# Spreading the middle stage of long convolutions through an attention, with loads a task ahead and stores a task late

## The chip, the cores and the metric

The kernel runs on one core of a Trainium2 chip. The core has a matrix engine (TensorE, PE in the profile; its weight loads are shown as PEld), a vector engine (VectorE, DVE), a scalar engine (ScalarE, ACT), a general engine (GpSimd, POOL) and SyncE (SP), which here only issues DMA transfers. Each engine works through its own queue in order, and semaphores let one wait for another. Products accumulate in PSUM banks of 128 × 512 numbers of 32 bits, working tiles lie in SBUF, everything else in the chip's DRAM. The metric is the device time of one execution, in microseconds; less is better.

## The reference

One encoder layer on 2048 rows of 1024 numbers. The input is projected; a part of the columns goes to an attention of 8 heads, another to a "Hyena" group, which passes a sequence twice through a long two-sided filter and a gate. Both results are normalised, put side by side and projected again; routed experts follow.

```python
def attend(blk):
    qn, qr = blk
    s = jnp.einsum('bqhd,bkhd->bhqk', qn, k_nope) + jnp.einsum('bqhr,bkr->bhqk', qr, k_rope)
    p = jax.nn.softmax(s.astype(jnp.float32) * scale, axis=-1).astype(v.dtype)
    return jnp.einsum('bhqk,bkhd->bqhd', p, v)
...
for o in range(HYENA_ORDER):
    zf = z.astype(jnp.float32)
    y = jnp.fft.irfft(jnp.fft.rfft(zf, n=2 * S, axis=1) * filt_f[:, o], n=2 * S, axis=1)[:, :S]
    z = (parts[o + 1].astype(jnp.float32) * (y + zf * hyena_bias[o])).astype(hy_raw.dtype)
```

The change touches only how these two are laid side by side. What is computed stays the same.

## The kernel before, in words

**The attention** (`attention`) goes through 32 blocks: 8 heads, each in 4 quarters of 512 queries. A block (a round, below) is 16 steps, one for each 128 keys. A step makes the scores (three products, `s`), two exponentials on ScalarE (`eh`, and the full value over `s`), the remainder `el` on VectorE, a sum over steps on GpSimd (`acc`), and two products with the values (`o`, `l`) for the step two before. In between stands work for the next block: one or two `max_step`, each a product `x` and a maximum on VectorE (`mx`), 16 in a block; at step 14 `max_row`, which reduces these maxima to one number for a query (`nm`), copies it to column 96 of `mz`, transposes `mz` with four products and has ScalarE put the row into the next block's queries; and at step 9 `query`, the queries of the block after the next. `free_sums` and `close_block` end the block before at steps 1 and 3. The next block's scores need the row that `max_row` makes.

**The convolutions** (`hyena`, one generator) run beside it: at each step of the attention it gets 0.7 of a turn (`drive`), and one PSUM bank, `h`. Each of the two orders `o` has four kinds of tasks, over two halves `i` of the channels: `spectrum` (the filter's spectrum, `F_dr`), `fwd1` (first products of the transform, into `Ad`), a middle stage (`first_half`: products with `zm`, the multiplication with the spectrum on VectorE (`pr`) and GpSimd (`zs`, `y`); `second_half`: products with `ivm`, into `Bd`), and `inv` (last products and the gate `tb`, into `Z1` or `HY`). The order is plain: all of `spectrum`, all of `fwd1`, the whole middle stage of both halves, all of `inv`, and the same for the second order. Each task issues its loads where it starts and its store where it ends, on SyncE's queue.

**What sets the order on an engine.** The code is written in the order of these turns, and a scheduler places the instructions of each engine from it, with the buffers and banks as limits. So instructions written apart can stand side by side in the end. Tiles named `ta`, `tb`, `tc` are the convolutions' three kinds of buffers (3, 2 and 2 of each).

Of the kernel before, what the change touches and what calls it, by code (L numbers as in the profile page):

```python
# [11 lines left out]
F32 = mybir.dt.float32  # L12
# [36 lines left out]
def hybrid_layer(ctx, tc, I, out):  # L49
# [581 lines left out]
    def hyena(hp, hw, bk):  # L631
# [7 lines left out]

        def fwd1(o, i, q4):  # L640
# [3 lines left out]
            zt = hw.tile([128, 4, HC], F32, name="tb")  # L644
            SY.dma_start(zt, ZS[o][:, q4 * 4:q4 * 4 + 4, hc])
            for q2 in range(2):
                ev = hw.tile([128, 2, 2, HC], F32, name="tc")
                for qq in range(2):
                    ql = q2 * 2 + qq
                    p = bk("h")  # L650
                    for mt in range(2):
                        T.matmul(p[:, mt * HC:(mt + 1) * HC], w1c[:, ql, mt * 128:mt * 128 + 128], zt[:, ql, :],
                                 start=True, stop=True)
                    A.activation(ev[:, :, qq, :], p.rearrange("p (m c) -> p m c", m=2), AF.Copy)
                    if qq == 0:
                        yield
                for mt in range(2):
                    q0 = q4 * 4 + q2 * 2
                    SY.dma_start(Ad[2 * o + i][mt * 128:mt * 128 + 128, q0:q0 + 2, :], ev[:, mt])
                yield  # L660

        def spectrum(o, g4):
            kt = hw.tile([128, 4, CH], F32, name="tc")
            SY.dma_start(kt, pat(Af[o], g4 * 4 * 128 * CH, [[CH, 128], [128 * CH, 4], [1, CH]]))
            for g2 in range(2):
                ev = hw.tile([128, 2, CH], F32, name="ta", bufs=3)
                for gg in range(2):
# [3 lines left out]
                    if gg == 0:  # L671
                        yield
                g0 = g4 * 4 + g2 * 2
                SY.dma_start(F_dr[o][g0:g0 + 2].rearrange("g p c -> p g c"), ev)
                yield

        def first_half(o, i, g4):
            hc = slice(i * HC, (i + 1) * HC)
            kt = hw.tile([128, 4, HC], F32, name="ta", bufs=3)
            SY.dma_start(kt, pat(Ad[2 * o + i], g4 * 4 * 128 * HC, [[HC, 128], [128 * HC, 4], [1, HC]]))  # L680
            ff = hw.tile([128, 4, 2, HC], F32, name="tc")
            for hh in range(2):
                SY.dma_start(ff[hh * 64:hh * 64 + 64], pat(F_dr[o], g4 * 4 * 128 * CH + i * HC,
                                                           [[CH, 64], [128 * CH, 4], [64 * CH, 2], [1, HC]]))
            ys = YS[g4] = []
            for g2 in range(2):
                gs = slice(g2 * 2, g2 * 2 + 2)
                p = bk("h")
# [1007 lines left out]
```

## Time and profile before

| | us |
|---|---|
| median of 3 runs | 3455.32 (3454.94 to 3457.93) |
| profiled execution | 3456.35 |
| its span, first to last instruction | 3454.6 |
| first and last product of `s` (line 866) | 661.3 and 1865.6 |
| first products of the next stage (`mm`, line 73) | 1951.5 |

TensorE is busy 93% of the span, VectorE 67%, ScalarE 49%, GpSimd 42%; the mean granted clock of TensorE is 0.958. The page divides the span into 40 slices of 86 us; the attention is in slices 8 to 21, counted from 0. A line such as `L803 PE MATMUL x<-kh,qt` is an instruction of line 803 on TensorE that writes `x` from `kh` and `qt`; the name after `<-` in square brackets in a timeline is what ended the idle time before it. Products with 32-bit operands appear as two records each.

### The profile page before, as it was taken

Reading aid. Unit: us, or ns where it says so; the run is one execution under the profiler, and the core shown is the slowest. Engines: PE = TensorE matmul, PEld = TensorE weight load, DVE = VectorE, ACT = ScalarE, POOL = GpSimd, SP = SyncE. Lnnn points to the kernel's source line nnn. Section 1 sums busy time; section 2 is a strip of 40 time slices with the busy share of each in tenths; the row PEclk is TensorE's granted clock in tenths of the full one; section 3 lists DMA queues with packets and bytes.
Section 4 is the critical chain, followed back from the end, with each engine's and each line's share of the span. In section 5 each row is a group of like instructions: output and inputs, shape, how many; then the busy total and the mean of one; then the engine's idle time right before and its main releaser. Section 6 shows DMA issues by size and latency. Waiting matters only on the chain.

```text
span 3454.6 us, 41964 instructions
## 1 busy us (share of the span) xinstructions
PE 3196.6 (93%) x14790; PEld 2477.7 (72%) x14790; DVE 2301.5 (67%) x3528; ACT 1697.8 (49%) x2569; POOL 1456.5 (42%) x1134
## 2 busy tenths in 40 slices
PE   7899999899989999999998699599999999999897
PEld 3667787666767776677776488477788877887676
DVE  7975343776677776667774377776656566565886
ACT  4762222566667664667774244233444344444442
POOL 5750000556678784658886266300100010000564
PEclk9999999699999999999999899799999999999998
DMA  6444353356466467647456643455666566665784
GB/s 192 158 150 118 111 145 94 97 175 175 156 162 150 108 160 236 176 165 163 119 126 194 222 155 131 150 171 186 215 199 203 183 217 210 208 203 186 268 279 160
DMA packets 373755, 594.16 MB, mean 172 GB/s; under 512 B 36859, under 2 KB 190013, under 8 KB 373097
## 3 DMA queue, kind: packets, MB, share of 16 engines
q1 hardware_dynamic: 347097, 528.95, 48.5%
q0 software_dynamic: 26304, 62.00, 7.1%
q8 instruction: 117, 1.92, 0.2%
q14 instruction: 93, 0.76, 0.1%
q10 hardware_dynamic: 144, 0.52, 0.0%
HBM read 438.84 MB, written 152.58 MB: 171 GB/s over the span
## 4 chain that ended last, share of the span: by engine, by line
PE 70%; DVE 11%; DMA 8%; issue 4%; POOL 3%; ACT 3%; SPq 0%; POOLq 0%; DVEq 0%; ACTq 0%
PE g L73 9%; PE g L74 9%; PE g L75 8%; PE s L866 3%; PE s L867 3%; PE s L868 3%; PE o L859 3%; PE l L860 3%; PE x L803 3%; PE mm L75 3%; PE mm L74 3%; PE mm L73 3%; DMA w<-in_w_ada_dram 3%; PE h L669 2%; PE h L716 1%
## 5 line engine op out<-in xcount | busy, mean ns | idle before, releaser
L881 POOL TENSOR_TENSOR acc<-acc,eh 128x512 f32<-128x512 f32 x480 | 615.8, 1283 | 157.3 <-ACT eh L874 132.3
L65 DVE TENSOR_TENSOR wl<-raw,wh 128x2048 fp32r<-128x2048 f32 (+1 forms) x210 | 473.3, 2256 | 225.0 <-ACT wh L59 224.0
L59 ACT ACTIVATE wh<-raw 128x2048 fp32r<-128x2048 f32 x192 | 367.5, 1915 | 439.9 <-PE g L75 341.4
L65 DVE TENSOR_TENSOR el<-s,eh 128x512 fp32r<-128x512 f32 x512 | 349.2, 687 | 158.2 <-ACT s L875 153.2
L805 DVE TENSOR_REDUCE mx<-x 128x1 f32<-128x512 f32 x512 | 346.4, 685 | 140.5 <-PE x L803 138.1
L73 PE MATMUL g<-wh,xh 128*128 128x512 f32 x1024 | 411.1, 402 | 3.2 <-DVE xh L62 2.3
L74 PE MATMUL g<-wl,xh 128*128 128x512 f32 x1024 | 408.3, 399 | 1.6 <-DVE wl L65 1.5
L75 PE MATMUL g<-wh,xl 128*128 128x512 f32 x1024 | 407.5, 398 | 1.0 <-DVE xl L65 1.0
L874 ACT ACTIVATE eh<-s 128x512 fp32r<-128x512 f32 x512 | 304.9, 596 | 205.1 <-PE s L868 179.0
L1495 POOL DMA_INDIRECT ACC<-ye,idx x30 | 65.8, 2195 | 691.0 <-DVE ye L1486 565.5
L875 ACT ACTIVATE s<-s 128x512 f32<-128x512 f32 x512 | 304.5, 595 | 0.0
L860 PE MATMUL l<-el,vt 128*66 128x512 f32 x512 | 226.5, 446 | 0.6 <-DVE acc L820 0.4
L73 PEld LDWEIGHTS g<-wh,xh 128*128 128x128 f32 x1024 | 193.0, 188 | 47.0 <-DVE xh L62 3.1
L74 PEld LDWEIGHTS g<-wl,xh 128*128 128x128 f32 x1024 | 193.1, 189 | 45.4 <-DVE wl L65 2.7
L75 PEld LDWEIGHTS g<-wh,xl 128*128 128x128 f32 x1024 | 192.7, 188 | 45.7 <-DVE xl L65 1.8
L803 PE MATMUL x<-kh,qt 96*128 96x512 f32 x512 | 221.9, 446 | 1.8 <-DVE mx L805 1.6
L866 PE MATMUL s<-qt,kh 97*128 97x512 f32 x512 | 214.9, 420 | 3.3 <-ACT qt L815 2.7
L73 PE MATMUL mm<-uT,wh 128*128 128x512 f32 x512 | 207.8, 407 | 5.4 <-DVE uT L62 5.4
L73 PE MATMUL g<-wh,hh 128*128 128x512 f32 x512 | 205.9, 403 | 5.8 <-ACT hh L59 5.8
L74 PE MATMUL g<-wl,hh 128*128 128x512 f32 x512 | 205.9, 402 | 5.2 <-DVE wl L65 5.2
L867 PE MATMUL s<-qt,kh 96*128 96x512 f32 x512 | 208.2, 407 | 0.0
L868 PE MATMUL s<-qt,kh 96*128 96x512 f32 x512 | 207.2, 405 | 0.0
(408 smaller groups left out, 6988.9 us busy)
## 6 DMA issues: line engine op xcount, KB each, us to landing
raw<-in_w_gate_dram SPq DMA_DIRECT2D x64, 1024.0 KB, 5.0
raw<-in_w_up_dram SPq DMA_DIRECT2D x64, 1024.0 KB, 7.1
raw<-in_w_down_dram SPq DMA_DIRECT2D x64, 1024.0 KB, 10.1
tc<-F_dr SPq DMA_DIRECT2D x64, 512.0 KB, 5.2
w<-in_w_ada_dram SPq DMA_DIRECT2D x48, 512.0 KB, 4.4
Af<-ev SPq DMA_DIRECT2D x32, 512.0 KB, 2.6
tc<-Af SPq DMA_DIRECT2D x16, 1024.0 KB, 6.4
F_dr<-ta SPq DMA_DIRECT2D x32, 512.0 KB, 3.0
```

The costliest lines, as they stand in the source:

```text
L59: return A.activation(hi, src, AF.Copy)
L65: return eng.tensor_tensor(lo, src, hi.bitcast(F32), OP.subtract)
L73: first = T.matmul(o, wh, xh, start=start, stop=False)
L74: T.matmul(o, wh, xl, start=False, stop=False)
L75: T.matmul(o, wl, xh, start=False, stop=stop)
L803: T.matmul(p, qh[0:96, i * 128:i * 128 + 128], khs[h % 2][0:96, 0, c * 512:c * 512 + 512], start=True, stop=True)
L805: V.tensor_reduce(mx[:, i, c:c + 1], p, axis=AX.X, op=OP.max)
L860: T.matmul(pl[0:66], vt[:, k, 64:130], el, start=k == 0, stop=k == NT - 1)
L866: T.matmul(p, kh[0:97, ks], qh[0:97, :], start=True, stop=False)
L867: T.matmul(p, kh[0:96, ks], ql[0:96, :], start=False, stop=False)
L868: T.matmul(p, kl[0:96, ks], qh[0:96, :], start=False, stop=True)
L881: G.tensor_tensor(acc, acc, eh.bitcast(F32), OP.add)
```

## The change

`first_half` and `second_half` become one task, `mid`, which makes the first half of a group and the second half of the group before. Every task is now a generator whose first part only issues loads. A list of tasks is laid out in which the middle stage of one half of the channels is spread between tasks of other kinds of the other half or of the next order (`spread`). The loop over the list starts the loads of the next task and issues the stores of the last one at the first turn of a task. In the attention `max_row` moves to step 12 and its transposes, now `set_row`, to step 14; the products with the values are put off at a block's start (the first at step 3), `close_block` moves to step 5 and its store (`keep`) to step 7; the steps with two `max_step` change from 7 and 10 to 2, 6 and 11; steps 5 and 9 give the convolutions no turn, the others 0.8. `mz` is 98 columns wide instead of 128, `tb` has 3 buffers.

```diff
+        def mid(o, i, g4):
...
+            yield
+            done = YS.pop((i, g4 - 1), None)
+            if done:
+                bt = hw.tile([128, 4, HC], F32, name="tb", bufs=3)
+            if g4 < 8:
+                ys = YS[i, g4] = []
             for g2 in range(2):
...
+                    G.tensor_tensor(zs, zs, ff[:, gs, 1], OP.mult)
+                    y = hw.tile([128, 2, HC], F32, name="y", bufs=4)
+                    G.tensor_tensor(y, pr, zs, OP.add)
+                    ys += [y[:, 0], y[:, 1]]
+                    yield
+                if done:
+                    pi = bk("h")
...
+                    A.activation(bt[:, g2 * 2:g2 * 2 + 2, :], pi.rearrange("p (g c) -> p g c", g=2), AF.Copy)
+                    yield
+            if done:
+                stores.append((pat(Bd[2 * o + i], (g4 - 1) * 4 * 128 * HC, [[HC, 128], [128 * HC, 4], [1, HC]]), bt))
...
             w2i = hw.tile([128, 4, 2, 128], F32, name="ta", bufs=3)
             SY.dma_start(w2i, I["k_w2i"][:, q4 * 1024:q4 * 1024 + 1024].rearrange("p (q k m) -> p q k m", q=4, k=2))
-            gt = hw.tile([128, 4, HC], F32, name="tb")
+            b2 = hw.tile([128, 2, 4, HC], F32, name="tc")
+            SY.dma_start(b2, Bd[2 * o + i][:, qs, :].rearrange("(k p) q c -> p k q c", k=2))
+            gt = hw.tile([128, 4, HC], F32, name="tb", bufs=3)
             SY.dma_start(gt, HZ[1 + o][:, qs, hc])
+            yield
             for q2 in range(2):
-                b2 = hw.tile([128, 2, 2, HC], F32, name="tc")
...
-            SY.dma_start(ZO[o][:, qs, hc], gt)
...
+            stores.append((ZO[o][:, qs, hc], gt))
+
+        YS, stores = {}, []
+
+        def spread(mids, others, lead):
+            mids, others = list(mids), list(others)
+            for k in range(lead):
+                yield mids[k]
+            n = len(mids) - lead
+            for k in range(n - 1):
+                yield from others[k * len(others) // (n - 1):(k + 1) * len(others) // (n - 1)]
+                yield mids[lead + k]
+            yield mids[-1]
...
+        nine = range(9)
+        tasks = [*group(fwd1, 0, 0), *group(spectrum, 0),
+                 *spread(group(mid, 0, 0, n=nine), group(spectrum, 0, n=range(4, 8)) + group(fwd1, 0, 1), 1),
+                 *spread(group(mid, 0, 1, n=nine), group(inv, 0, 0) + group(fwd1, 1, 0) + group(spectrum, 1), 2),
+                 *spread(group(mid, 1, 0, n=nine), group(spectrum, 1, n=range(4, 8)) + group(inv, 0, 1)
+                         + group(fwd1, 1, 1), 2),
+                 *spread(group(mid, 1, 1, n=nine), group(inv, 1, 0, n=range(2)), 2),
+                 *group(inv, 1, 0, n=range(2, 4)), *group(inv, 1, 1)]
+        next(tasks[0])
+        for n, t in enumerate(tasks):
+            late, stores[:] = list(stores), []
+            for k, _ in enumerate(t):
+                if k == 0:
+                    for d, src in late:
+                        SY.dma_start(d, src)
+                    if n + 1 < len(tasks):
+                        next(tasks[n + 1])
+                yield
...
         def max_row(n):
-            qh, ql, mx = blk[n]
+            mx = blk[n][2]
             nm = aw.tile([128, 4], F32R, name="nm")
             V.tensor_reduce(nm, mx, axis=AX.X, op=OP.max, negate=True)
             V.tensor_copy(mz[:, :, 96], nm.bitcast(F32))
+
+        def set_row(n):
+            qh = blk[n][0]
             p = bk("x")
             for i in range(4):
-                T.transpose(p[:, i * 128:i * 128 + 128], mz[:, i, :], ident)
+                T.transpose(p[0:98, i * 128:i * 128 + 128], mz[:, i, :], ident)
             A.activation(qh[96:97, :], p[96:97, :], AF.Copy)
...
+                for g in {0: (-2,), 1: (-1,), 2: (), 3: (0,), 4: (1, 2)}.get(k, (k - 2,)):
+                    if g >= 0 or n > 0:
+                        pv(n + g // 16, g % 16)
...
+                if n + 1 < NB:
+                    if k == 12:
+                        max_row(n + 1)
+                    if k == 14:
+                        set_row(n + 1)
+                yield k not in (5, 9)
...
-        drive(itertools.islice(at, 12), hy, 1.5)
-        drive(at, hy, 0.7, -1.0)
+        credit = 0.0
+        for n, free in enumerate(at):
+            credit += free * (1.5 if n < 12 else 0.8)
+            while credit >= 1.0:
+                credit -= 1.0
+                next(hy, None)
         drive(hy)
```

**How the instructions stand.** Blocks are counted from 0. The first place is the end of block 24. `o`, `l`, `x`, `s` are the attention's products, `h` those of the convolutions. On TensorE before, from the last but one maximum's product:

```order
L803 MATMUL x<-kh_4448,qt 128x512
L859 MATMUL o<-eh,vt_4458 128x512
L860 MATMUL l<-el,vt_4458 66x512
L803 MATMUL x<-kh_4448,qt 128x512
L691 MATMUL h<-ta,zm 128x256 x2
L860 MATMUL l<-el,vt_4458 66x512
L814 MATMUL x<-ident,mz 128x128 x4
L803 MATMUL x<-kh_4448,qt 128x512
L716 MATMUL h<-y,ivm 128x256 x2
L866 MATMUL s<-qt,kh_4448 128x512
```

and with the change:

```order
L815 MATMUL x<-kh_4448,qt 128x512 x2
L875 MATMUL l<-el,vt_4458 66x512
L874 MATMUL o<-eh,vt_4458 128x512
L652 MATMUL h<-tb,ta 128x256 x2
L875 MATMUL l<-el,vt_4458 66x512
L815 MATMUL x<-kh_4448,qt 128x512
L652 MATMUL h<-tb,ta 128x256 x4
L829 MATMUL x<-ident,mz 98x128 x4
L815 MATMUL x<-kh_4448,qt 128x512
L652 MATMUL h<-tb,ta 128x256 x2
L887 MATMUL s<-qt,kh_4448 128x512
```

Between the last product of a maximum and the transposes of `mz` stood one batch for the middle stage and one `l`; now there is one batch of `fwd1`. The transposes, two steps behind `max_row` in the code, stand at the end of the block in both, in front of the next block's scores.

VectorE at the same place before (`mx` maxima, `osb` parts of `free_sums`, `pr` the middle stage's):

```order
L65 TENSOR_TENSOR el<-s,eh 128x512
L805 TENSOR_REDUCE mx<-x 128x1 x2
L695 TENSOR_TENSOR pr<-h,tc 128x512
L810 TENSOR_REDUCE nm<-mx 128x4
L821 TENSOR_TENSOR osb<-o,osb 64x512
L811 COPY mz<-nm 128x4
L822 TENSOR_TENSOR osb<-o,osb 64x512
```

and with the change:

```order
L65 TENSOR_TENSOR el<-s,eh 128x512 x2
L817 TENSOR_REDUCE mx<-x 128x1 x3
L836 TENSOR_TENSOR osb<-o,osb 64x512
L822 TENSOR_REDUCE nm<-mx 128x4
L837 TENSOR_TENSOR osb<-o,osb 64x512
L823 COPY mz<-nm 128x4
L835 TENSOR_TENSOR acc<-l,acc 1x512
```

The copy into `mz` still follows the last maximum by two other instructions; the middle stage's `pr` has given way to a part of `free_sums`.

The second place is GpSimd's queue in block 21, where `spectrum` and `fwd1` ran before (`qf`, `qt` belong to `query`):

```order
L879 TENSOR_SCALAR acc<-eh 128x512
L881 TENSOR_TENSOR acc<-acc,eh 128x512 x13
L348 TENSOR_TENSOR qf<-qf,osb 32x512
L881 TENSOR_TENSOR acc<-acc,eh 128x512
L65 TENSOR_TENSOR qt<-qf,qt 96x512
L881 TENSOR_TENSOR acc<-acc,eh 128x512
```

and with the change:

```order
L899 TENSOR_SCALAR acc<-eh 128x512
L901 TENSOR_TENSOR acc<-acc,eh 128x512 x8
L706 TENSOR_TENSOR zs<-zs,tc 128x512
L901 TENSOR_TENSOR acc<-acc,eh 128x512
L708 TENSOR_TENSOR y<-pr,zs 128x512
L901 TENSOR_TENSOR acc<-acc,eh 128x512 x4
L706 TENSOR_TENSOR zs<-zs,tc 128x512
L901 TENSOR_TENSOR acc<-acc,eh 128x512
L348 TENSOR_TENSOR qf<-qf,osb 32x512
L708 TENSOR_TENSOR y<-pr,zs 128x512
L901 TENSOR_TENSOR acc<-acc,eh 128x512
L65 TENSOR_TENSOR qt<-qf,qt 96x512
```

Two `zs` and two `y` of the middle stage have come between the sums, the last `y` close to the block's end.

The third place is TensorE at the end of the attention before (`tr`: transposes of the next stage):

```order
L859 MATMUL o<-eh,vt_4459 128x512 x2
L860 MATMUL l<-el,vt_4459 66x512 x2
L736 MATMUL h<-tc,ta 128x256 x4
L859 MATMUL o<-eh,vt_4459 128x512
L860 MATMUL l<-el,vt_4459 66x512
L736 MATMUL h<-tc,ta 128x256 x4
L829 MATMUL x<-ones,acc 128x1 x4
L831 MATMUL x<-ident,osb 128x64 x4
L736 MATMUL h<-tc,ta 128x256 x48
L1009 MATMUL tr<-ident,at 128x128 x4
L1009 MATMUL tr<-ident,hy 128x128 x4
```

and with the change:

```order
L874 MATMUL o<-eh,vt_4459 128x512 x2
L875 MATMUL l<-el,vt_4459 66x512 x2
L736 MATMUL h<-tc,ta 128x256 x4
L874 MATMUL o<-eh,vt_4459 128x512
L875 MATMUL l<-el,vt_4459 66x512
L736 MATMUL h<-tc,ta 128x256 x4
L844 MATMUL x<-ones,acc 128x1 x4
L846 MATMUL x<-ident,osb 128x64 x4
L736 MATMUL h<-tc,ta 128x256 x28
L1041 MATMUL tr<-ident,at 128x128 x4
L1041 MATMUL tr<-ident,hy 128x128 x4
```

Behind the last products of the attention (L831, now L846) 48 products of `inv` stood; now there are 28.

## Rows read from the trace of the kernel before

**Rows 1.** The page: busy time; TensorE's busy tenths and granted clock in 40 slices.

```profile
PE 3196.6 (93%) x14790; PEld 2477.7 (72%) x14790; DVE 2301.5 (67%) x3528; ACT 1697.8 (49%) x2569; POOL 1456.5 (42%) x1134
...
PE   7899999899989999999998699599999999999897
...
PEclk9999999699999999999999899799999999999998
```

**Rows 2.** Windows: stretch, length; PE, PEld, DVE, ACT, POOL busy; clock, DMA share, GB/s.

```profile
656.80:769.20 112.40, 105.04 (x419) 77.80 (x420) 86.55 (x143) 77.41 (x148) 67.27 (x54) 0.93 0.41 138
769.20:990.90 221.70, 214.90 (x910) 157.79 (x910) 152.30 (x248) 151.09 (x282) 138.82 (x114) 1.00 0.61 177
990.90:1262.10 271.20, 247.04 (x1064) 193.62 (x1064) 206.19 (x320) 185.44 (x344) 231.40 (x189) 0.94 0.53 126
1262.10:1397.30 135.20, 124.52 (x511) 93.61 (x512) 86.86 (x141) 65.47 (x122) 71.97 (x58) 0.95 0.74 221
1397.30:1583.00 185.70, 179.35 (x768) 133.27 (x767) 128.47 (x210) 126.64 (x235) 117.22 (x96) 1.00 0.58 174
1583.00:1873.10 290.10, 274.23 (x1210) 215.45 (x1210) 210.33 (x343) 205.80 (x379) 253.52 (x209) 0.96 0.56 136
1873.10:1931.60 58.50, 32.90 (x96) 22.86 (x96) 8.23 (x14) 0.00 (x0) 2.92 (x3) 0.80 0.80 264
1931.60:1951.50 19.90, 1.97 (x8) 1.57 (x8) 2.16 (x4) 3.08 (x6) 0.24 (x1) 0.60 0.93 336
```

**Rows 3.** Waits of TensorE, 640 to 1880: us in total, times, longest us.

```profile
PE x L814 <- DVE mz L811: 29.9, 15, 5.3
PE h L652 <- ACT tc L654: 7.0, 13, 1.5
PE h L669 <- ACT ta L670: 5.3, 11, 0.7
...
PE h L736 <- DMA tc<-Bd: 3.2, 2, 2.3
...
PE h L669 <- DMA tc<-Af: 2.6, 1, 2.6
```

**Rows 4.** Tile mz, the copies: ns min/median/max, first and last start.

```profile
L811 DVE COPY mz<-nm x32: 152/208/4784, 656.8 to 1838.9; 128x4 f32<-128x4 f32 x32
```

**Rows 5.** Timeline, end of a block: start us, us, engine, instruction, [idle before].

```profile
1618.64 1.09 PE L691 MATMUL h<-ta,zm 128*128 128x256 f32 x4
...
1618.77 1.28 DVE L805 TENSOR_REDUCE mx<-x 128x1 f32<-128x512 f32 x2
...
1621.30 0.79 DVE L811 COPY mz<-nm 128x4 f32<-128x4 f32 x1
...
1622.15 0.66 PE L814 MATMUL x<-ident,mz 128*128 128x128 f32 x4 [2.18 <-DVE mz L811]
```

**Rows 6.** Timeline of GpSimd and VectorE at the longest copy.

```profile
990.78 1.25 POOL L881 TENSOR_TENSOR acc<-acc,eh 128x512 f32<-128x512 f32 x1
...
994.44 1.25 POOL L704 TENSOR_TENSOR zs<-zs,tc 128x512 f32<-128x512 f32 x1
...
990.94 4.78 DVE L811 COPY mz<-nm 128x4 f32<-128x4 f32 x1
```

**Rows 7.** Chain of waits: a half task of `inv` inside the attention.

```profile
1858.62 1.73 PE h L736 x8
```

**Rows 8.** Waits of TensorE, 1873 to 1952.

```profile
PE tr L1009 <- DMA at<-AO: 17.9, 1, 17.9
PE h L736 <- DMA tc<-Bd: 15.8, 7, 4.0
PE h L736 <- DVE tb L739: 9.8, 5, 6.6
```

**Rows 9.** Timeline: a half task in the tail whose load is there.

```profile
1908.90 1.99 PE L736 MATMUL h<-tc,ta 128*128 128x256 f32 x8 [0.78 <-DVE tb L739]
```

**Rows 10.** Waits of SyncE's queue, 640 to 1950.

```profile
SPq L683 <- POOL zs L704: 75.7, 26, 6.4
```

**Rows 11.** The page's DMA issues: KB each, median us to landing.

```profile
tc<-F_dr SPq DMA_DIRECT2D x64, 512.0 KB, 5.2
```

More of the change, by code (lines that the diff above doesn't have):

```diff
@@ L742, in inv @@
-            SY.dma_start(ZO[o][:, qs, hc], gt)
-        YS = {}
-        def turns(*gens):
-            gens = list(gens)
-            while gens:
-                for g in list(gens):
-                    if next(g, gens) is gens:
-                        gens.remove(g)
-                    else:
-                        yield
-        for o in range(2):
-            for g4 in range(8):
-                yield from spectrum(o, g4)
-            for i in range(2):
-                for q4 in range(4):
-                    yield from fwd1(o, i, q4)
-            for i in range(2):
-                yield from first_half(o, i, 0)
-                for g4 in range(1, 9):
-                    yield from turns(second_half(o, i, g4 - 1), *([first_half(o, i, g4)] if g4 < 8 else []))
-            for i in range(2):
-                for q4 in range(4):
-                    yield from inv(o, i, q4)
-                    yield
+                yield
@@ new lines, in inv, with group @@
+            stores.append((ZO[o][:, qs, hc], gt))
[9 more added lines that the diff above has]
+            yield mids[-1]
+        def group(f, *a, n=range(4)):
+            return [f(*a, k) for k in n]
@@ L771, in attention @@
+        next(tasks[0])
[7 more added lines that the diff above has]
+                        next(tasks[n + 1])
+                yield
+        for d, src in stores:
+            SY.dma_start(d, src)
+        yield
     def attention(kp, aw, bk):
-        mz = kp.tile([128, 4, 128], F32, name="mz")
+        mz = kp.tile([128, 4, 98], F32, name="mz")
@@ L836, in close_block, with keep @@
                             rc[:, :, None].to_broadcast([128, 4, 64]), OP.mult)
+            return oo
+        def keep(n, oo):
+            h, b = divmod(n, 4)
             (G if n == NB - 1 else SY).dma_start(AO[:, b * 4:b * 4 + 4, h * 64:h * 64 + 64], oo)
@@ L843, in attention, with pv @@
             max_step(0, j)
[L844 removed]
+            yield 1
         max_row(0)
[L846 removed]
+        set_row(0)
+        live, done = {}, {}
+        def pv(n, k):
+            if k == 0:
+                live[n] = bk("o"), bk("l")
+            po, pl = live[n]
+            eh, el = ph.pop((n, k))
+            vt = vts[n // 4 % 2]
+            T.matmul(po, vt[:, k, 0:128], eh, start=k == 0, stop=k == NT - 1)
+            T.matmul(pl[0:66], vt[:, k, 64:130], el, start=k == 0, stop=k == NT - 1)
+        ph, accs = {}, {}
         for n in range(NB):
             h, b = divmod(n, 4)
[L849 to L850 removed]
             qh, ql, _ = blk[n]
[L852 to L862 removed]
+            kh, kl = khs[h % 2][:, 0], khs[h % 2][:, 1]
+            acc = accs[n] = aw.tile([128, 512], F32, name="acc")
+            maxes = iter(range(16 if n + 1 < NB else 0))
             for k in range(NT):
```

152 lines of the change are left out of this document (58 added, 94 removed).

## The prediction

> **What bounds the kernel now.** Read the page's shares first, then the slices, then the stages one by one. TensorE is busy for 93% of the span, and its row of slices holds 9s except in a few places [rows 1]. So no other engine sets the time, and a change is worth what it takes from TensorE in one of three forms: work, idle time, or time at a lower granted clock. The attention with the convolutions beside it runs from about 657 to 1873 us, and the edit touches only that stage and the short stretch behind it. I cut it at the copies into mz, of which there is one for each of the 32 rounds (a head's quarter, 16 steps) [rows 2]. For each stretch I count as lost: length minus TensorE's busy time, plus (1 − granted clock) × length.
>
> - first rounds (three): 7.4 + 0.07 × 112.4 = 15.2 us
> - spectrum and first products beside attention, 6 rounds: 6.8 + 0 = 6.8 us
> - middle stage, 7 rounds: 24.2 + 0.06 × 271.2 = 40.4 us
> - change to the last products and back, 3 rounds: 10.7 + 0.05 × 135.2 = 17.4 us
> - spectrum and first products again, 5 rounds: 6.4 us
> - middle stage again, 8 rounds: 15.9 + 0.04 × 290.1 = 27.5 us
>
> Together 113.7 us. A light round loses 13.2 / 11 = 1.2 us, a round beside the middle stage 67.9 / 15 = 4.5 us. The list of waits names why: 29.9 us in 15 waits are the four transposes of mz waiting for VectorE's copy [rows 3]. One such end of a round [rows 5]: the last maximum's product is issued before 1618.64, TensorE then has only two products of the convolution and one l product, while VectorE still does mx, pr, nm, osb and the copy; the transposes start 2.18 us late at 1622.15, and everything behind them (the next round's scores need the row they make) is late with them. The copy itself has a median of 0.21 us and a maximum of 4.78 [rows 4]. The long one began at 990.94 while GpSimd was in an addition, went on beside four of its instructions and ended at 995.72, when the last of them ended [rows 6]. GpSimd is busy 0.63 of the light stretch and 0.85 to 0.87 of the middle ones [rows 2], so there it is seldom free.
>
> The Trainium skill (SBUF — State Buffer, "Who interferes with whom") says that a VectorE copy that uses two ports and a GpSimd instruction exclude each other for one whole instruction. This row agrees that the copy waits and differs in how long: it waited out four, not one. By the rule a copy would lose at most one addition, 1.25 us in that row, and the 11 light rounds, which get GpSimd work of the middle stage after the change, at most 14 us.
>
> Behind the attention comes the tail: from 1873.1 to 1931.6 us TensorE does 96 records, 12 half tasks of the last products (`inv`), at 58.5 / 12 = 4.88 us each although one is 1.73 us of products in the attention [rows 7]; it waits 15.8 us for loads of Bd and 9.8 for VectorE's gate [rows 8], the DMA engines being 0.80 busy at 264 GB/s. Then 17.9 us pass until the next stage has its first rows [rows 8].
>
> **The change part by part.** Counts of instructions on TensorE, VectorE, ScalarE and GpSimd are the same; SyncE issues 48 DMAs fewer of the same bytes (stores of Ad and loads of Bd come in one where there were two). SyncE gets one new thing to wait for: a load a task ahead stands in its queue until the buffer of two tasks ago is read out, and the stores behind it stand too. Such waits were there before (75.7 us in 26 for GpSimd's zs, 6.4 the longest [rows 10]). A task has four turns, at 11.2 turns a round of some 36 us about 13 us; a wait of 6.4 us and a load of 5.2 [rows 11] fit into it, so I cost it at nothing; if they don't fit, the products of the next task wait as they did at the change of stage.
>
> 1. The tail. In the change's order 28 products stand behind the last of the attention where 48 stood: 7 half tasks for 12. At the old pace this saves 5 × 4.88 = 24.4 us. The load of the next task now stands ahead of the current one's products, so some of the 25.6 us of waiting goes too. The floor is the pace of a half task whose load is there, 1.99 + 0.78 us [rows 9]: 7 × 2.77 = 19 us, a saving of 39. The volume a task moves is unchanged and the engines were 0.80 busy, so I take a point nearer the old pace: 29 us for the seven, a saving of 29.5. The 17.9 us behind stay: those loads are issued after the last store, as before.
> 2. The 20 products moved forward are now done inside the attention: 5 × 1.73 = +8.7 us.
> 3. The waits inside the attention. Three edits act on them. (a) `max_row` moves to step 12 and the transposes, as `set_row`, to step 14. This looks as if it parted copy and transposes, but the order shows that the scheduler brings them together again: at the end of round 24 one batch of convolution products stands between the last maximum and the transposes, as before. I cost this edit at nothing. (b) The middle stage's share of each round halves and reaches nearly all rounds from the fifth on, so GpSimd has about the same share everywhere: (138.8 + 231.4 + 72.0 + 117.2 + 253.5) / 1103.9 = 0.74 of the time from 769 to 1873. (c) Loads a task ahead: the waits at the change of stage, such as 3.2 us for Bd and 2.6 for Af [rows 3], lie now under other tasks; these three rounds lost 17.4 us. What is late next is again mz, on TensorE and through VectorE's queue: behind a waiting copy stand the el and mx of the next round, and TensorE's l and x products wait for those.
>  No row shows a round with half a middle stage. The nearest rows are the light round, 1.2 us, and the middle round, 4.5 us; halfway is 2.85. Of the middle's 67.9 us 27.9 are clock, which the light stretches at 1.00 don't lose at all, so shorter waits cost less than their share: that speaks for less than halfway. The order leaves TensorE two convolution products or none as cover in about half the rounds: that speaks against much less. I take 2.4. With 29 rounds and the first three as before: 29 × 2.4 + 15.2 = 84.8 us lost, against 113.7: −28.9. The bounds: 1.2 gives 50 us (−64), 4.5 gives 145.7 (+32).
> 4. Heavy steps (5 and 9) give no convolution turn, at 0.8 a turn instead of 0.7: 14 × 0.8 = 11.2 turns a round, and 16 × 0.7 = 11.2 before. Nothing. Later closing of a block (steps 3 and 5 for 2 and 3) only moves products within a round: nothing; it costs if ScalarE must wait for a buffer of eh that the later products still hold.
> 5. Smaller transposes of mz: 98 instead of 128 columns held as weights, the moved side is unchanged; nothing.
>
> Sum: −29.5 + 8.7 − 28.9 = −49.7 us. The profiled execution took 3456.35 us (span 3454.6), so 3406.7; the median of the runs is 1.0 lower: 3406.
>
> **The rivals.**
> - *Every round becomes a middle round.* Place: the copy into mz at the end of each round. If half the middle stage is enough to keep GpSimd in additions at that moment, all 29 rounds lose 4.5 us; the tail saves only its count (24.4). 3455.3 + 32 + 8.7 − 24.4 = 3472, slower. It decides from 3.9 us a round on: 29 × 3.9 + 15.2 + 8.7 − 24.4 = 113. For it: GpSimd's order now has zs and y in round 21, which had none, and in light rounds TensorE's waits were for ScalarE's tc and ta, 7.0 and 5.3 us [rows 3], hardly for mz. Against it: the share of 0.74, and that the 64 zs and 64 y (2 in each of 8 tasks, of 2 halves, of 2 orders) are spread over some 27 rounds instead of 16.
> - *The waits are only shared out.* Rounds lose 3.4 us on average, as over these 29 rounds now: only tail and moved products count, 3455.3 − 29.5 + 8.7 = 3434. For it: the cover beside the transposes in the order is no larger than before. Against it: the stage changes are gone and a short wait leaves the clock alone (the light stretches show 1.00), so several waits under 2 us cost less than one of 5 us.
> - *All rounds become light.* 1.2 us each and a tail near its floor: 3455.3 − 64 + 8.7 − 34 = 3366. For it: the light rounds hold 11 turns too. Against it: those have no work on GpSimd but the sums.
> - *The change doesn't take hold in the tail*, because the last task's Bd store and load lie right at the end: then 12 half tasks' worth of time stays, 3455.3 − 28.9 = 3426 or so; it lies inside the range.
>
> **How the numbers follow.** Forecast (1.8 to 3 us a round, 3390 to 3425): 0.52. Waits only shared out, or no gain in the tail (3425 to 3448): 0.24. All rounds light (below 3390): 0.14. Every round a middle round (above 3448): 0.10, of which 0.06 is slower. About 0.2%, 7 us, is what a measurement of this kernel can tell from no change: faster by more 0.90, within 0.04, slower 0.06. The range takes 1.5 us a round with a saving of 39 in the tail (−55 + 8.7 − 39) to some 3.5 with 24.4 (+3 + 8.7 − 24.4): 3372 to 3442.
>
> **What would show it.** Right: the tail from the last product of the attention to the next stage's first transposes falls from 76 (58.5 + 17.9) to about 47 us with 56 records of `inv` in it; no wait for Bd or Af of over 1 us inside the attention; the wait of the transposes for mz at 25 to 45 us in more but shorter pieces, and a granted clock of 0.97 or more in every stretch of the attention; GpSimd at 0.70 to 0.80 in all of them. Wrong: copies into mz of 2 us and more in many rounds with the clock at 0.95 or less behind them (first rival); or a new wait on TensorE for VectorE's mx or el inside the rounds, which would mean that the later query has moved the queue of maxima to the end of the round and VectorE sets its length.

## The result, and the profile after

The changed kernel takes 3402.6 us (median of 4 runs, 3401.0 to 3406.1) beside 3456.6 of the kernel before (3454.9 to 3458.7): ratio 0.9845, 95% interval 0.9828 to 0.9862. Medians here and below leave out two runs (3635.4 us of the kernel before, 3611.1 us of the version max_late), which took about 5% longer at a granted clock of 0.83. The profiled execution took 3403.19 us with a span of 3401.4, which is 53.2 less than before.

Where they went, by the same marks as in the prediction: the attention, from its first copy into mz to its last product, went from 1216.3 to 1198.5 us (-17.8, although it now holds 40 more records of `inv`); the tail went from 58.5 to 27.4 (-31.1); the wait behind it from 17.9 to 18.1; and the kernel behind that wait, which the change doesn't touch, from 1505.1 to 1500.7. What stands ahead of the first copy took 656.8 us and 656.7. Over all profiled runs of this study the part behind lies between 1498.0 and 1505.6 and the part ahead between 651.5 and 657.5, without any relation to the edits, so the last 4.4 us are scatter.

The page: busy time, and TensorE's slices, in answer to [rows 1].

```profile
PE 3177.4 (93%) x14790; PEld 2466.7 (73%) x14790; DVE 2286.6 (67%) x3528; ACT 1700.0 (50%) x2569; POOL 1459.6 (43%) x1134
...
PE   7899999999999999999999799599999999999897
...
PEclk8999999699999999999999899799999999999999
```

The work is the same, only the places where TensorE stands have changed. The windows, cut at the same copies as [rows 2] (stretch, length; PE, PEld, DVE, ACT, POOL busy; clock, DMA share, GB/s):

```profile
656.70:762.60 105.90, 100.20 (x411) 75.18 (x411) 85.18 (x142) 75.02 (x144) 66.43 (x54) 0.94 0.37 125
762.60:989.30 226.70, 213.97 (x899) 155.49 (x900) 157.51 (x258) 156.76 (x290) 158.34 (x130) 1.00 0.64 174
989.30:1254.80 265.50, 253.62 (x1124) 199.66 (x1124) 190.14 (x309) 176.58 (x326) 198.87 (x162) 0.97 0.61 168
1254.80:1368.20 113.40, 107.24 (x448) 79.71 (x448) 77.78 (x128) 77.39 (x144) 82.29 (x67) 0.97 0.52 140
1368.20:1555.70 187.50, 179.06 (x766) 133.82 (x766) 136.44 (x224) 128.93 (x238) 144.46 (x119) 0.99 0.71 187
1555.70:1856.00 300.30, 284.54 (x1277) 224.39 (x1278) 213.41 (x346) 199.48 (x369) 230.93 (x191) 0.98 0.61 167
```

Counted as in the prediction (idle plus clock), the stretches lose 12.1, 12.7, 19.9, 9.6, 10.3 and 21.8 us, together 86, against 113.7. So the 11 rounds that were light lose 23.0 where they lost 13.2, the 15 that stood beside the middle stage 41.7 where they lost 67.9, and the three at the change of stage 9.6 for 17.4. GpSimd is busy for 0.70 to 0.77 of the last five stretches.

The waits of TensorE in the attention, in answer to [rows 3], and the copies, in answer to [rows 4]:

```profile
PE x L829 <- DVE mz L823: 16.0, 16, 3.6
...
PE h L715 <- ACT zs L701: 10.5, 6, 2.2
...
PE h L667 <- ACT ta L668: 5.9, 9, 2.0
...
PE h L736 <- DMA tc<-Bd: 1.1, 1, 1.1
...
PE h L667 <- DMA tc<-Af: 0.6, 1, 0.6
```

```profile
L823 DVE COPY mz<-nm x32: 156/426/4146, 656.7 to 1820.2; 128x4 f32<-128x4 f32 x32
```

The wait for mz has nearly halved. The median copy is longer than before (0.43 us for 0.21), but only one is held for over 1.5 us, where three were (4.78, 3.57 and 3.31 us).

The tail, waits and four of TensorE's rows, in answer to [rows 8, 9] ("issue" is idle time for which the profile shows no cause):

```profile
PE tr L1041 <- DMA at<-AO: 18.1, 1, 18.1
PE h L736 <- issue: 5.2, 1, 5.2
PE h L736 <- DVE tb L741: 3.5, 4, 1.1
PE h L736 <- DMA tc<-Bd: 1.1, 1, 1.1
```

```profile
1855.33 1.99 PE L736 MATMUL h<-tc,ta 128*128 128x256 f32 x8
...
1868.37 3.75 PE L736 MATMUL h<-tc,ta 128*128 128x256 f32 x8 [5.20 <-issue]
...
1880.57 1.99 PE L736 MATMUL h<-tc,ta 128*128 128x256 f32 x8 [0.79 <-DVE tb L741]
...
1900.71 1.12 PE L1041 MATMUL tr<-ident,at 128*128 128x128 f32 x4 [18.14 <-DMA at<-AO]
```

The 1.1 us for Bd is the one wait for Bd in both lists; it lies at 1857, behind the attention. The 56 records (seven half tasks) take 27.4 us, 3.9 each where it was 4.88.

### The profile page after: what moved, and what is told of

Its sections match the earlier page's. It is cut to its first block, busy times and chain, and to the rows that moved or that the text cites. A ratio compares the mean times of both kernels' runs of the same rounds, so it can differ in the third digit from the quotient of the medians.

```text
span 3401.4 us, 41832 instructions
## 1 busy us (share of the span) xinstructions
PE 3177.4 (93%) x14790; PEld 2466.7 (73%) x14790; DVE 2286.6 (67%) x3528; ACT 1700.0 (50%) x2569; POOL 1459.6 (43%) x1134
## 4 chain that ended last, share of the span: by engine, by line
PE 72%; DVE 11%; DMA 7%; issue 4%; POOL 3%; ACT 3%; SPq 0%; POOLq 0%; DVEq 0%; ACTq 0%
PE g L73 9%; PE g L74 9%; PE g L75 9%; PE s L887 3%; PE s L888 3%; PE mm L75 3%; PE s L889 3%; PE mm L74 3%; PE mm L73 3%; PE x L815 3%; PE o L874 3%; PE l L875 3%; DMA w<-in_w_ada_dram 2%; PE h L736 2%; PE h L652 2%
## 5 line engine op out<-in xcount | busy, mean ns | idle before, releaser
L1527 POOL DMA_INDIRECT ACC<-ye,idx x30 | 67.9, 2263 | 687.7 <-DVE ye L1518 565.3
L75 PEld LDWEIGHTS g<-wh,xl 128*128 128x128 f32 x1024 | 193.3, 189 | 45.5 <-DVE xl L65 1.4
L815 PE MATMUL x<-kh,qt 96*128 96x512 f32 x512 | 211.3, 441 | 3.9 <-DVE mx L817 2.4
L73 PE MATMUL mm<-uT,wh 128*128 128x512 f32 x512 | 208.1, 408 | 5.3 <-DVE uT L62 5.3
L74 PE MATMUL mm<-uT,wh 128*128 128x512 f32 x512 | 206.7, 404 | 1.1 <-DVE uT L65 0.7
L75 PE MATMUL mm<-uT,wl 128*128 128x512 f32 x512 | 205.6, 402 | 0.0
```

The costliest lines, as they stand in the source:

```text
L73: first = T.matmul(o, wh, xh, start=start, stop=False)
L74: T.matmul(o, wh, xl, start=False, stop=False)
L75: T.matmul(o, wl, xh, start=False, stop=stop)
L815: T.matmul(p, qh[0:96, i * 128:i * 128 + 128], khs[h % 2][0:96, 0, c * 512:c * 512 + 512], start=True, stop=True)
```

## The experiments

All ratios are to the kernel before, timed on the same chip (its medians: 3454.6 beside attn_only to row_together, 3457.4 beside before_red to pv_old, 3451.5 beside the last four). "Loss" is TensorE's idle time plus (1 - clock) x length, from the first copy into mz to the last product of the attention, with the clock averaged over that whole stretch and not rounded; so counted it is 111.6 us before and 84.0 after. It comes from one profiled run of each kernel. "Held" counts copies into mz of over 1.5 us. The tail is TensorE's records of the convolutions behind that stretch, and its length.

| kernel | median us | ratio | idle + clock = loss | held | tail: records, us |
|---|---|---|---|---|---|
| before | 3456.6 | 1 | 71.2 + 40.4 = 111.6 | 3 | 96, 58.5 |
| after | 3402.6 | 0.9845 | 60.6 + 23.4 = 84.0 | 1 | 56, 27.4 |
| attn_only | 3441.3 | 0.9965 [0.9951, 0.9979] | 78.6 + 34.9 = 113.5 | 5 | 64, 40.8 |
| conv_only | 3432.4 | 0.9935 [0.9914, 0.9956] | 71.9 + 45.7 = 117.6 | 2 | 72, 32.7 |
| old_order | 3409.1 | 0.9881 [0.9853, 0.9909] | 61.8 + 20.6 = 82.4 | 5 | 72, 39.7 |
| row_together | 3396.6 | 0.9839 [0.9812, 0.9866] | 61.7 + 23.2 = 84.9 | 1 | 56, 26.7 |
| before_red | 3421.8 | 0.9908 [0.9893, 0.9923] | 58.5 + 15.6 = 74.1 | 0 | 96, 58.4 |
| after_red | 3392.6 | 0.9815 [0.9801, 0.9830] | 54.2 + 15.4 = 69.6 | 0 | 56, 27.0 |
| no_ahead | 3410.2 | 0.9854 [0.9834, 0.9875] | 64.8 + 25.7 = 90.5 | 1 | 56, 27.1 |
| pv_old | 3415.9 | 0.9878 [0.9861, 0.9895] | 69.3 + 30.1 = 99.4 | 2 | 56, 27.2 |
| conv_only_red | 3419.0 | 0.9907 [0.9888, 0.9926] | 62.2 + 30.2 = 92.4 | 0 | 72, 32.9 |
| old_order_red | 3380.7 | 0.9786 [0.9767, 0.9805] | 41.0 + 10.3 = 51.3 | 0 | 72, 37.9 |
| max_late | 3428.5 | 0.9926 [0.9906, 0.9946] | 68.3 + 24.9 = 93.2 | 3 | 112 (96 of inv), 55.9 |
| pv_max_old | 3417.0 | 0.9895 [0.9874, 0.9916] | 66.3 + 36.1 = 102.4 | 3 | 100 (96 of inv), 46.1 |

The whole stretch in the kernels on which the argument rests, in this order: before, after, old_order, before_red, after_red, conv_only_red, old_order_red (columns as in the windows above; here the clock is rounded):

```profile
656.80:1873.10 1216.30, 1145.09 (x4881) 871.54 (x4881) 870.71 (x1397) 811.85 (x1508) 880.20 (x718) 0.97 0.57 157
656.70:1855.20 1198.50, 1137.95 (x4921) 867.62 (x4921) 859.83 (x1402) 814.15 (x1508) 881.32 (x718) 0.98 0.60 165
656.70:1849.70 1193.00, 1131.11 (x4905) 860.89 (x4905) 872.07 (x1400) 814.31 (x1508) 879.28 (x718) 0.98 0.60 164
654.20:1838.10 1183.90, 1125.41 (x4881) 857.34 (x4881) 851.98 (x1397) 811.37 (x1508) 881.43 (x718) 0.99 0.58 161
652.50:1839.60 1187.10, 1132.92 (x4921) 863.08 (x4921) 848.68 (x1402) 813.97 (x1508) 881.49 (x718) 0.99 0.61 167
656.70:1863.90 1207.20, 1145.02 (x4906) 869.23 (x4906) 852.38 (x1400) 810.78 (x1508) 881.84 (x717) 0.97 0.58 162
655.20:1821.40 1166.20, 1125.15 (x4905) 857.54 (x4905) 845.02 (x1401) 814.38 (x1508) 879.36 (x718) 0.99 0.61 167
```

**The two halves of the change.** attn_only: the kernel before with the new `attention` and the new turns.

```diff
-        drive(itertools.islice(at, 12), hy, 1.5)
-        drive(at, hy, 0.7, -1.0)
+        for n, free in enumerate(at):
+            credit += free * (1.5 if n < 12 else 0.8)
+            ...
```

> The attention's edits and the new turns alone, beside the convolutions as they were. My theory: the gain inside the attention comes from spreading the middle stage, so the attention's rounds lose about as much as before (114 us); in the order 44 products of inv stand behind the attention instead of 48, one half task less: 3456 - 4.9 + 1.7 = 3453, between 3440 and 3460. Rival: the attention's edits (copy and transposes parted in the code, later closing of a block) bring the gain inside the attention: losses near 85 us, 3424.

Measured 3441: the theory's loss (113.5 us) is right; the tail was shorter than expected (8 half tasks at 5.1 us), so the time lies at the low end. The attention's edits alone take nothing from the loss, with five copies held.

conv_only: the new convolutions (one-batch turns, loads ahead, late stores, the spread order) with the old `attention` and turns, mz 98 wide to make room.

> The convolutions' edits alone (tasks spread, loads a task ahead, stores late), beside the attention and the turns as they were; only mz is 98 wide, for room. My theory: losses inside the attention fall to about 85 us (-29), the 44 products left behind it go at the new pace of 3.9 us a half task: 11 x 3.9 = 43 us instead of 58.5, + 1.7 us moved: 3456 - 29 - 15.5 + 1.7 = 3413. Rival: without the attention's edits the losses stay at 114 us: 3442.

Measured 3432: the theory fell. The loss is 118 us although the middle stage is spread; what is gained is the tail. So neither half lowers the loss alone.

**The spread alone.** old_order: the changed kernel with its tasks in the order of before.

```diff
-        tasks = [*group(fwd1, 0, 0) ... spread(...) ...]
+        for o in range(2):
+            tasks += group(spectrum, o, n=range(8)) + group(fwd1, o, 0) + group(fwd1, o, 1)
+            tasks += group(mid, o, 0, n=nine) + group(mid, o, 1, n=nine) + group(inv, o, 0) + group(inv, o, 1)
```

> The changed kernel with its tasks in the order of before (all spectrum, all first products, the middle stage of both halves, inv), loads still a task ahead and stores late, the attention's edits kept. My theory: the rounds beside the middle stage lose some 4 us each again, only the waits at the changes of stage go: about 100 us lost; 36 products behind the attention, 9 half tasks of 3.9 us: 3456 - 14 - 23.4 + 5.2 = 3424. Rival: loads ahead and the attention's edits are what counts, not the order of tasks: near the changed kernel plus one and a half half tasks, 3408.

Measured 3409, the rival's number: with the middle stage back in two blocks the loss is 82 us, no more than after. The spread's worth is the tail, 39.7 against 27.4 us; in the whole time the intervals of the two ratios overlap.

**The split of the row's maximum.** row_together: `max_row` and `set_row` both at step 14.

> The changed kernel with max_row and set_row both at step 14. My theory: the scheduler brings copy and transposes together anyway, so nothing changes: 3403, within 6 us. Rival: the two steps between them are what shortened the waits for mz (29.9 to 16.0 us, with less clock lost behind them): 3425.

The order on every engine is that of the changed kernel, and the ratio is the same within its interval: costing this edit at nothing was right.

**The held copy, taken away.** In four kernels the copy into mz became a reduction over one element, with the same result and at the same place in VectorE's order:

```diff
-            V.tensor_copy(mz[:, :, 96], nm.bitcast(F32))
+            V.tensor_reduce(mz[:, :, 96], nm.bitcast(F32)[:, :, None], axis=AX.X, op=OP.max)
```

> The kernel before, in which the row's maxima are brought into mz by a reduction over one element instead of by a copy (same values, same place in VectorE's order; the products and ScalarE's and SyncE's work stand in the same order). Theory (VectorE's copies into mz are what GpSimd's additions hold up; the reduction just ahead of them never took more than 0.17 us in 32): the new instruction takes about 0.2 us each time, TensorE's wait for mz falls from 29.9 to under 12 us, and part of the clock's 40 us comes back with it: the loss inside the attention falls from 114 to about 85 us, 3425 us (3415 to 3435) against 3456, ratio 0.991. Rival (the transposes wait for VectorE's whole chain of maxima, pr and osb; the copy is only its last link): the wait moves to another instruction or stays, loss 108 to 118, 3450 to 3460, ratio 0.999.

> The changed kernel with the same exchange of copy for reduction; the order on every engine is that of the changed kernel. Theory (the copy is held by GpSimd): 16.8 us of copies fall to 5, TensorE's wait for mz from 16.0 to under 8 us, the clock's loss from 23 to some 18: loss 84 to about 71, 3390 us (3384 to 3396) against 3403, ratio 0.981 to the kernel before. Rival (what is left of the wait is VectorE's chain): 3399 to 3405, ratio 0.984.

Both theories hold within 4 us in the time: 3422 for 3425 and 3393 for 3390. In before_red the loss falls further than expected (74.1 us for 85) and the wait for mz a little less (13.6 us for under 12); in after_red that wait is 8.7 us for under 8. The tile mz in before_red (ns min/median/max) and TensorE's wait for it:

```profile
L811 DVE TENSOR_REDUCE mz<-nm x32: 141/145/161, 654.2 to 1803.9; 128x4 f32<-128x4 f32 x32
```

```profile
PE x L814 <- DVE mz L811: 13.6, 11, 2.0
```

The held copies cost the kernel before 111.6 - 74.1 = 37.5 us and the changed kernel 84.0 - 69.6 = 14.4. So of the 27.6 us by which the loss fell, 23 are holding of copies that no longer occurs and 4.5 are other losses. These sums count somewhat too much: the stretch itself became 32.4 and 11.4 us shorter by the exchange, and 2.5 and 2.8 us of the two falls lie in the first round, where no copy was held. Their difference stays near 21 to 23 us either way.

> The new convolutions with the old attention (as in conv_only, 3432), with the reduction in place of the copy into mz; same order. Theory (the edits of the attention and of the convolutions change the loss inside the attention only by how often TensorE is caught without cover behind a held copy; without the copy all versions lose 70 to 75 us): the loss falls from 118 to about 75 us, 3432 - 42 = 3390 us (3384 to 3400), ratio 0.981, beside after_red's 0.9815. Rival (the old attention loses more by itself): the loss falls by the 16 us of copies only, to about 100, 3416 us (3408 to 3424).

The rival is right: 92 us of loss stay in the new convolutions beside the old attention, 18 more than in before_red and 23 more than in after_red.

> The changed kernel with its tasks in the order of before (old_order, 3409), with the reduction in place of the copy. Theory (all versions lose 70 to 75 us without the held copy): the loss falls from 82 to about 70 us, 3409 - 12 = 3397 us (3391 to 3402), ratio 0.983; the spreading is then worth 4 us or less to a kernel whose copies are not held. Rival (its 33 us of copies come back whole): 3376 us (3370 to 3385), ratio 0.977, the fastest of all.

The rival's mechanism (all the holding comes back: 31.1 us of loss) and the lowest time of all, 3381 us; beside after_red, run on another chip, the intervals of the ratios still just overlap (0.9786 and 0.9815). One round shows the price of one held copy. Ahead of it VectorE, GpSimd and TensorE stand in the same order in both kernels; first the timeline of old_order (start us, us, engine, instruction, [idle before]):

```profile
1697.42 1.26 POOL L898 TENSOR_TENSOR acc<-acc,eh 128x512 f32<-128x512 f32 x1
...
1697.96 0.69 DVE L834 TENSOR_TENSOR osb<-o,osb 64x512 f32<-64x512 f32 x1
...
1698.58 5.01 DVE L820 COPY mz<-nm 128x4 f32<-128x4 f32 x1
1698.65 1.26 POOL L706 TENSOR_TENSOR zs<-zs,tc 128x512 f32<-128x512 f32 x1
...
1702.31 1.25 POOL L898 TENSOR_TENSOR acc<-acc,eh 128x512 f32<-128x512 f32 x1
...
1703.65 1.09 PE L826 MATMUL x<-ident,mz 128*98 128x128 f32 x4 [4.17 <-DVE mz L820]
```

and the same place in old_order_red:

```profile
1681.47 0.69 DVE L834 TENSOR_TENSOR osb<-o,osb 64x512 f32<-64x512 f32 x1
...
1682.08 0.15 DVE L820 TENSOR_REDUCE mz<-nm 128x4 f32<-128x4 f32 x1
1682.14 1.26 POOL L706 TENSOR_TENSOR zs<-zs,tc 128x512 f32<-128x512 f32 x1
...
1682.83 1.06 PE L826 MATMUL x<-ident,mz 128*98 128x128 f32 x4
```

The copy begins while GpSimd is in an addition and ends at 1703.59, when the fourth instruction behind that one ends; the reduction doesn't wait. The windows of this round, and of the light rounds and the second middle stage, old_order first:

```profile
1371.80:1523.40 151.60, 146.99 (x625) 108.40 (x626) 98.57 (x166) 105.16 (x192) 91.18 (x74) 1.00 0.56 174
1523.40:1812.60 289.20, 271.04 (x1204) 211.84 (x1204) 226.30 (x355) 207.59 (x384) 251.72 (x207) 0.98 0.57 139
1698.60:1739.50 40.90, 36.45 (x155) 28.44 (x155) 30.71 (x45) 26.00 (x48) 32.98 (x28) 0.92 0.47 112
```

```profile
1356.40:1508.00 151.60, 146.98 (x625) 108.38 (x625) 98.52 (x165) 105.17 (x192) 91.14 (x74) 1.00 0.56 174
1508.00:1784.30 276.30, 267.91 (x1206) 210.04 (x1205) 214.09 (x356) 207.60 (x384) 251.82 (x207) 0.99 0.60 145
1682.10:1718.10 36.00, 35.64 (x155) 28.09 (x155) 25.81 (x44) 25.99 (x48) 32.88 (x28) 0.95 0.53 125
```

The round takes 40.9 us with the copy and 36.0 with the reduction. The light rounds are alike within 0.05 us on every engine. The eight rounds beside the middle stage lose 8.4 us idle and 0.01 of the clock without a held copy, 18.2 and 0.02 with the two that are held there, at the same 251.8 us of GpSimd (0.91 of the time without, 0.87 with). Taken round by round that is 1.3 us a round without the held copies, beside 1.15 in a light one. So a busy GpSimd alone costs TensorE next to nothing here; a copy that it holds does. In the kernel before it costs more: the fifteen rounds beside the middle stage lose 2.3 us each in before_red, where no copy is held, beside 1.2 in a light one.

**Loads a task ahead.** no_ahead: the changed kernel with the loads at a task's own first turn.

```diff
-        next(tasks[0])
-        ...
-                    if n + 1 < len(tasks):
-                        next(tasks[n + 1])
+            next(t)
```

> The changed kernel in which a task's loads are issued at its own first turn instead of a task ahead; its stores still go out at the start of the next task, and the order of tasks, the attention's edits and the 28 products in the tail stay. Theory (loads ahead are what took the waits of the convolutions' products and the clock's losses out of the rounds): the loss inside the attention goes back from 84 to 105 to 115 us and the tail's pace from 3.9 to about 4.9 us a half task: 3403 + 26 + 7 = 3436 us (3425 to 3445). Rival (loads ahead count in the tail only, inside the attention the loads are hidden anyway): loss 80 to 90, 3403 + 7 = 3410 (3404 to 3416).

Measured 3410, the rival's time, but not in its place: the tail is as fast as after, 27.1 us, and the loss rises to 90.5. The intervals of this kernel and of after overlap, so the loads ahead are worth some microseconds at most.

**The edits of the attention, one by one.** pv_old puts the last two steps' products of o and l back into their own round; max_late puts the second maxima back to steps 7 and 10 and both halves of the row's maximum to 14; pv_max_old does both.

```diff
-                for g in {0: (-2,), 1: (-1,), 2: (), 3: (0,), 4: (1, 2)}.get(k, (k - 2,)):
+                for g in range(max(k - 2, 0), k - 1):
```

```diff
-                for j in itertools.islice(maxes, 2 if k in (2, 6, 11) else 1):
+                for j in itertools.islice(maxes, 2 if k in (7, 10) else 1):
```

> The changed kernel in which the last two steps' products of o and l stand at the end of their own round again, and the first of a round start at its third step, as before; the earlier maxima, the turns and the convolutions stay. Theory (products kept back over the edge of a round are cover for the transposes of mz, and with them the new convolutions get by on fewer waits): the loss inside the attention rises from 84 to 100 to 115 us, 3403 + 22 = 3425 us (3415 to 3435). Rival (the cover does not matter; it is the earlier maxima or the turns): loss 80 to 90, 3399 to 3408 us.

> The changed kernel with the steps' second maxima at steps 7 and 10 instead of 2, 6 and 11, and the row's maximum with the transposes at step 14, as before: the last maximum comes a step later. The order leaves 48 products of the convolutions in the tail (28 in the changed kernel): 12 half tasks at the changed kernel's 3.9 us each less 8.7 us of products that leave the attention make 3403 + 20 - 9 = 3414 us by themselves. Theory (the earlier maxima give the held copy time before it is needed, the half of the loss that the products over the edge don't explain): the loss inside the attention is 95 to 110 us and the time 3432 us (3422 to 3442). Rival (the place of the maxima doesn't matter): loss 80 to 90, 3410 to 3418 us.

> The changed kernel with both edits undone: the products of o and l in their own round (as in pv_old, loss 99) and the maxima late (as in max_late); 48 products in the tail. What is left of the attention's edits are the turns and the later closing. Theory (these two edits are what conv_only lacks): the loss is 110 to 120 us as in conv_only, 3403 + 31 + 11 = 3445 us (3436 to 3452). Rival (the products over the edge are all of it, or the turns): loss 95 to 103, 3430 us (3422 to 3436).

pv_old: 99 us of loss, 0.0033 of the ratio or 11 us more; the median of 3416 lies at the low end of the theory's range, the loss just under it. Of the 15.4 us of loss more, 10.7 stand in one round (13.8 us where the changed kernel loses 3.1), in which the copy into mz was held for 6.55 us. So what the edit costs by itself, without the copy, is not shown. The wait for mz, pv_old and then max_late:

```profile
PE x L829 <- DVE mz L823: 24.0, 17, 6.8
```

```profile
PE x L829 <- DVE mz L823: 33.5, 20, 5.1
```

max_late: 3428, inside the theory's range, but not by its sum: the loss rose by 9 us only (to 93), and 28.5 us stand in the tail. There sixteen records of the middle stage, which the expectation didn't count, take the first 11.8 us, and the twelve half tasks of `inv` behind them keep a pace of 3.7 us. pv_max_old: neither; the two edits don't add. Its median (3417) is below the ranges of theory and rival, and its profiled run was the slowest of its four (3430.6), so its 102 us are too many. Each of these edits also gives all five engines another order, in which other copies are held; single-run losses of such versions differ for that reason too, and I read no more from them than that the kernel is slower without either edit, max_late clearly, pv_old by intervals that just touch.

## Why the prediction was right, and which reason was not

The forecast was 3406 us and the run gives 3402.6, and its terms are nearly met one by one. One of the reasons under them failed. (By its own terms the lower end of the range is 3455.3 - 55 + 8.7 - 39 = 3370, not 3372; nothing hangs on it.)

- **Tail** (step 1, -29.5): -31.1. The seven half tasks took 27.4 us for 29; 18.1 us stay behind. In every version the tail goes by its count and a pace, 4.9 to 5.1 us a half task with the old convolutions and 3.6 to 4.4 with the new. Of the reason for the pace one half fell: the waits fell from 25.6 to 9.8 us, but they fall as far without the loads ahead (no_ahead, 9.4 us, 3.9 a half task). What else in the new tasks does it, the merged stores and loads perhaps, wasn't tried alone.
- **Products moved into the attention** (step 2, +8.7): the attention's length less its loss went from 1104.7 to 1114.5, +9.8.
- **Waits inside the attention** (step 3, -28.9): -27.6, 84.0 us of loss for 84.8. The number was met by luck: this is the step whose reason failed. It named (b), the spread: GpSimd's share falls to 0.74, so copies are held less, and rounds meet at 2.4 us. The share came (0.70 to 0.77), the number of long holds fell (3 to 1), and the copies' holding, short holds included, accounts for 23 us, as the pairs with the reduction show. But old_order reaches the same loss without the spread, with five held copies, and conv_only doesn't reach it with the spread. The spread does two things of the same size: it takes 31.1 - 14.4 = 16.7 us of held copies away (old_order less old_order_red; after less after_red), and it adds 69.6 - 51.3 = 18.3 us of other losses. About half of these, 9.4 us, lie in the eleven rounds that are light in old_order_red (15.9 us in all) and get work of the middle stage in after_red (25.2); the rest lies in other rounds, and no run shows why. I had counted a middle round's loss as GpSimd's share; without the held copy eight such rounds lose little more than light ones in old_order_red, and the fifteen of before_red 2.3 us each for 4.5.
 What lowered the loss instead are the attention's edits and the new tasks together: from 74.1 (before_red) to 51.3 (old_order_red) with no copy held in either. Between conv_only_red and after_red, which differ by the attention's edits and turns alone, the loss falls by 22.8 us (92.4 to 69.6), again with no copy held. So these edits, which steps 3a and 4 had put at nothing, lower the loss by themselves beside the spread convolutions; in the old order of tasks no run parts them from the new tasks. Of the 23 us from before_red to old_order_red some 9 lie in the three rounds at the change of stage (13.5 to 4.1 us), where (c) of the step had looked; attn_only, with no held copy there, loses 10.9 in them, so most of the 9 goes with the new tasks. That it is the loads ahead is not shown, since no run undoes them in that order. Twelve more lie in the rounds beside the middle stage. Which of the attention's edits does it stays open: pv_old and max_late give 15 and 9 us of loss back, held copies among them, and not in sum. That "later closing" only moves products within a round (step 4) was not so: the change carries the last two steps' products of o and l into the next round.
- **The split of the row's maximum** (step 3a, nothing): shown by row_together. **The turns' rate** (step 4, nothing) was not run; at 0.7, 0.9 or 1.0 a turn in place of 0.8 the program has the same instructions in the same order on every engine.
- **The signs.** Right: 56 records and 45.5 us (27.4 + 18.1) to the next stage's first transposes; no wait over 1 us for Bd or Af inside the attention; GpSimd's share in the last five stretches (in the first it is 0.63). Wrong: the wait for mz was to be 25 to 45 us in more pieces and is 16.0 in 16; and the clock is 0.97 or more in five stretches, not in the first, 0.94 (which step 3 had left as it was).
- **The rivals.** "Every round a middle round" rested on GpSimd's share and falls with (b): held copies are few, and a held copy, not the share, makes a round heavy. "Only shared out" came true for the spread itself, but not for the sum. The other two did not come: all light rounds would have lost 50 us, and the tail has 56 records.

## What to carry to other kernels

When one short instruction stands between two engines and its longest case is twenty times its median, exchange that instruction before moving the work around it: one line (before_red) gave three fifths of what the whole change gave (0.9908 against 0.9845), and the lowest time here, not clearly below after_red, is that of the change without its spread, with that line. Read an engine's busy share as a sign only: the same work of GpSimd went with a loss of about 1 or 2 us a round or with 8 or 9, by whether a copy was held at the edge. And test a reason by undoing it alone: a sum that comes out right can stand on a wrong one.

## What the runs showed of the hardware

A VectorE copy of 128x4 values that starts beside GpSimd's instructions can wait out several of them: 5.01 us over the rest of one and four more of 1.25 us each, in a train without gaps. A reduction of the same size never did: 128 in four kernels took 0.14 to 0.17 us, 76 of them begun while GpSimd was in an instruction. The Trainium skill (SBUF — State Buffer, "Who interferes with whom") has the copy wait for one instruction; the trace agrees on the wait, and in this row it lasts to the end of the train. That is not so in every row. In the kernel before, a copy that began at 1262.08 was over after 1.34 us, at the end of one GpSimd instruction, though the next followed without a gap:

```profile
1262.08 1.34 DVE L811 COPY mz<-nm 128x4 f32<-128x4 f32 x1
...
1262.11 1.28 POOL L881 TENSOR_TENSOR acc<-acc,eh 128x512 f32<-128x512 f32 x1
1263.33 1.27 POOL L704 TENSOR_TENSOR zs<-zs,tc 128x512 f32<-128x512 f32 x1
```

What decides between the two is not shown. The Trainium skill (VectorE: DVE Perf Modes, "The perf-mode tier table (the rule you actually need)") has the reduction in the 1x form alone, the copy also in faster ones; that is in keeping with the reduction's not waiting. The Trainium skill (VectorE: DVE Perf Modes, "Rules for kernel authors") calls the reduction the slowest operation and would have it restructured on a hot path; for 128x4 values beside a busy GpSimd the measurement says the opposite.
The clock goes with it: taking the held copies away brought 24.8 us of the kernel before's 40.4 us of clock loss back (15.6 left), more than the 12.7 us of idle time. The two are not quite additive, and some of it lies in the first round: the stretch became 32.4 us shorter.
